# DeltaNet query norms through VectorE block transposes, stacked meta values, and one meta product per attention head

## The chip, the cores and the metric

The kernel runs on one core of one Trainium2 chip. The metric is the device time of one launch in microseconds (us). The engines are named as the profile names them: PE (TensorE matmuls), PEld (its weight loads), DVE (VectorE), ACT (ScalarE), POOL (GpSimd) and SP (SyncE, which issues DMAs here).

## The reference, cut to what matters

One layer of a hybrid decoder: RMS norm, one combined input projection (2048 channels, 512 tokens and 16 meta tokens ahead of them), three token mixers on disjoint heads, a gate on each head, one output projection, a residual and a last norm. The change touches two of the mixers.

```python
q_dn = l2_normalize(to_heads(cq, DN_HEADS)) * DN_DK ** -0.5      # t * rsqrt(sum(t*t) + EPS)
k_dn = l2_normalize(to_heads(ck, DN_HEADS))
o_dn = gated_delta_rule_chunked(q_dn, k_dn, v_dn, log_a, beta)   # solves (I + A) per chunk
o_dn = gated_head_norm(o_dn, dz, dn_norm_w)                      # o * rsqrt(mean(o*o) + EPS) * w * silu(z)
...
logits = einsum('bhqd,bhkd->bhqk', q_i, k) + c_i[..., :, None] - c[:, :, None, :]
mask = (key_pos <= q_pos) & (key_pos >= PAD)                     # the 16 meta tokens are keys too
o_fox = einsum('bhqk,bhkd->bhqd', softmax(where(mask, logits, NEG)), v)
```

DeltaNet has 6 heads of 128 channels, the forgetting attention 5 heads of 128. A query's square sum over its 128 channels is needed per head and token: 6 x 512 numbers.

## The kernel before, in words

The input projection is one long stream of PE matmuls. Float32 weights arrive by DMA as `raw` tiles (128x1024), ACT rounds them to a high part (`whi`, the cast at L167), DVE subtracts to get the low part (`wlo`, the split at L168), and each 128x128 piece is multiplied three times (xh by whi, xl by whi, xh by wlo; L235). A block is one such tile against 512 token columns (24 matmuls) or against 528 in two halves (48). There are 131 such casts and splits. PE can't begin a block's `wlo` products before its split is done.

DeltaNet works in two groups g = 0 and 1 of H = 3 heads. For each group the program has `dn_keys` (L655-713), `dn_inverse` (L716 on), `dn_values` (L811), `dn_queries` and `dn_mix` (L835 on). Queries lie as `qT`, channels in the partitions, so the square sum of a query crosses partitions. Before, each of the four 128-token blocks transposed its three heads' queries on PE (`pq`, L878) and ACT squared the result with an accumulated sum (L881); then an Ln and an Exp gave the reciprocal (L935, L936). `dn_inverse` inverts 51 matrices of 32x32 by a chain of 60 small DVE steps (L737 a product, L741 an addition, in place in `ab`), writes the result out and reads it back in another layout by DMAs that ACT issues (L744, L745 to the scratch `sc`; L748, L750 back as `iv` and `xm`), transposes 32x32 blocks on DVE (L755), and goes on with small PE products (`pm` L761, `pl`, `pn`). `conv_silu` makes keys, values and queries: `pb` from PSUM (L356), a four-tap convolution on DVE (L600, L602), then `silu`: a clamp on POOL (L367), three ACT steps (L368 to L370) and a DVE product (L371). A gate head goes from PSUM through L385 and the same `silu`.

A forgetting-attention head adds the meta tokens' share to its output `pfo` last. Probabilities of the meta keys lie as `ptm` (ACT copies L1271), the values as `vm` inside the tile `fm` in a high and a low part, side by side (L1176, L1177), and two 128x512 matmuls add them (L1279).

The order on each engine is made when the program is built, by a list scheduler that runs over a modelled timeline. Casts and splits have high priority. Some pieces are pinned: `behind(mm, n)` puts a PE product behind the n-th next product of the stream, and a `waits` list puts DVE's transposes of the inverse (L755) behind a given split. Every engine then runs its list in order, so whatever stands behind a waiting instruction waits too.

Of the kernel before, what the change touches and what calls it, by code (L numbers as in the profile page):

```python
# [8 lines left out]
F32 = mybir.dt.float32  # L9
# [5 lines left out]
ALU = mybir.AluOpType  # L15
# [68 lines left out]
def tile_hybrid_trunk(ctx, tc, xT, x_first, w_first, xtok, mtok, w_gate, w_in, w_out, w_dn, consts, lmask, fin_w, out, dbg=None):  # L84
# [16 lines left out]
    def t15(name, shape=(P, H, P), dt=F32):  # L101
        return wk.tile(list(shape), dt, tag="t15", bufs=6, name=name)
# [532 lines left out]
    def dn_keys(g):  # L635
# [19 lines left out]
        G.memset(kdm, 0.0)  # L655
        anm = wk.tile([NM, H, NM], F32, tag="anm", bufs=1, name=f"anm{g}")
        atm = wk.tile([NM, H, NM], F32, tag="atm", bufs=1, name=f"atm{g}")
        cols = wk.tile([P, 4, 5, H], F32, tag="cols", name=f"cols{g}")
        nb2, br, nbg, tmp = (cols[:, i] for i in range(4))
        gcl = lambda b, j: gcol[:NM if b == 4 else P, b, 6 + H * g + j : 6 + H * g + j + 1]  # L660
        G.memset(sk, 1.0)
        for b in (4, 0, 1, 2, 3):
# [35 lines left out]
        for b in (4, 0, 1, 2, 3):  # L698
# [10 lines left out]
            for j in range(H):  # L709
                dst = an[:, b * H + j, :] if b < 4 else anm[:, j, :]  # L710
                V.scalar_tensor_tensor(out=dst, in0=pg[:r, j * r : (j + 1) * r], scalar=nb2[:r, b, j : j + 1],
                                       in1=e2[:r, j, :r], op0=ALU.mult, op1=ALU.mult)
        st.update(kT=kT, kd=kd, at=at, an=an, kdm=kdm, anm=anm, br=br, nbg=nbg)
        return st

    def dn_inverse(g, st):  # L716
# [93 lines left out]

    def dn_values(g, st):  # L811
        vp = six.tile([P, NN, P], F32, tag="six", name=f"vp{g}")
        vpm = t15(f"vpm{g}", (P, P))
        G.memset(vpm, 0.0)
        br = st["br"]
        for j in range(H):
            h = H * g + j
            v = row(f"v{h}")[:, :T]
            conv_silu(("dv", h), 12 + h, v)
            pv = psm.tile([P, 512], F32, tag="m", name=f"pv{h}")  # L820
            for b in range(NB):
                PE.transpose(pv[:, b * P : (b + 1) * P], v[:, bsl(b)], ident)
            for b in range(NB):
                V.tensor_scalar_mul(vp[:, b * H + j, :], pv[:, b * P : (b + 1) * P], br[:, b, j : j + 1])
            pv2 = psm.tile([P, 512], F32, tag="m", name=f"pvm{h}")
            PE.transpose(pv2[:NM, :P], v[:, 0:NM], ident)
            V.tensor_scalar_mul(vpm[32 * j : 32 * j + NM], pv2[:NM, :P], br[:NM, 4, j : j + 1])
        st.update(vp=vp, vpm=vpm)

    def dn_queries(g, st):  # L830
# [5 lines left out]
    def dn_mix(g, st):  # L836
# [14 lines left out]
        f_ = wk.tile([P, 2, NB, H], F32, tag="ff", name=f"ff{g}")  # L851
        egs, egls, ons = {}, {}, {}

        def gated(b):
            pt = psm.tile([P, 512], F32, tag="m", name=f"pt{g}{b}")
            for j in range(H):
                PE.transpose(pt[:, j * P : (j + 1) * P], ons[b][:, j, :], ident)
            for j in range(H):
                o = zs["dz", H * g + j][:, b * P : (b + 1) * P]
                V.scalar_tensor_tensor(out=o, in0=pt[:, j * P : (j + 1) * P], scalar=dnws[:, 0:1], in1=o,  # L860
                                       op0=ALU.mult, op1=ALU.mult)
# [9 lines left out]
        def scores(b):  # L871
            ts = bsl(b)
            p1 = psm.tile([P, 512], F32, tag="m", name=f"pa{g}{b}")
            p2 = psm.tile([P, 512], F32, tag="m", name=f"pq{g}{b}")
            for j in range(H):
                PE.matmul(p1[:, j * P : (j + 1) * P], kT[:, j, ts], qT[:, j, ts], start=True, stop=True)
            for j in range(H):
                PE.transpose(p2[:, j * P : (j + 1) * P], qT[:, j, ts], ident)  # L878
            for j in range(H):
                sq = wk.tile([P, P], BF16, tag="sq", name=f"sqq{g}{b}{j}")  # L880
                A.activation(sq, p2[:, j * P : (j + 1) * P], AF.Square, accum_out=sq_[:, b, j : j + 1])  # L881
            atb = at[:, b * H : b * H + H, :]
            V.tensor_tensor(out=atb, in0=p1[:, : H * P].rearrange("p (h d) -> p h d", h=H), in1=atb, op=ALU.mult)
            eg = t15(f"eg{g}{b}")
            nc.sync.dma_start(out=eg, in_=gd[6 + H * g : 6 + H * g + H, ts].partition_broadcast(P))
            A.activation(eg, eg, AF.Exp)
            egl = wk.tile([P, H], F32, tag="egl", name=f"egl{g}{b}")
            V.tensor_copy(egl, eg[:, :, P - 1])
            G.tensor_tensor(out=eg, in0=eg, in1=qT[:, :, ts], op=ALU.mult)
            egs[b], egls[b] = eg, egl  # L890

        scores(0)
        for b in range(NB):
            ts, eg, egl = bsl(b), egs[b], egls[b]
            pk = psm.tile([P, 512], F32, tag="m", name=f"pks{g}{b}")
            for j in range(H):
                mm = PE.matmul(pk[:, j * P : (j + 1) * P], kT[:, j, ts], sst[:, j, :], start=True, stop=True)
            soon(mm, b, 0)
            z = t15(f"zz{g}{b}")
            for j in range(H):  # L900
                V.scalar_tensor_tensor(out=z[:, j, :], in0=pk[:, j * P : (j + 1) * P], scalar=nbg[:, b, j : j + 1],
                                       in1=vp[:, b * H + j, :], op0=ALU.mult, op1=ALU.add)
            py = psm.tile([P, 512], F32, tag="m", name=f"py{g}{b}")
            for j in range(H):
                mm = PE.matmul(py[:, j * P : (j + 1) * P], uf[:, b * H + j, :], z[:, j, :], start=True, stop=True)
                if j == 0:
                    late(mm, b, 1)
            soon(mm, b, 1)
            y = t15(f"y{g}{b}")
            A.copy(y, py[:, : H * P].rearrange("p (h d) -> p h d", h=H))  # L910
            if b < NB - 1:
                pn = psm.tile([P, 512], F32, tag="m", name=f"psn{g}{b}")
                for j in range(H):
                    mm = PE.matmul(pn[:, j * P : (j + 1) * P], kd[:, b * H + j, :], y[:, j, :], start=True, stop=True)
                    if j == 0:
                        late(mm, b, 2)
                soon(mm, b, 2)
                sn = t15(f"sn{g}{b}")
                for j in range(H):
                    V.scalar_tensor_tensor(out=sn[:, j, :], in0=sst[:, j, :], scalar=egl[:, j : j + 1],  # L920
                                           in1=pn[:, j * P : (j + 1) * P], op0=ALU.mult, op1=ALU.add)
                scores(b + 1)
            if b:
                gated(b - 1)
            po = psm.tile([P, 512], F32, tag="m", name=f"po{g}{b}")
            for j in range(H):
                pj = po[:, j * P : (j + 1) * P]
                PE.matmul(pj, at[:, b * H + j, :], y[:, j, :], start=True, stop=False)
                PE.matmul(pj, eg[:, j, :], sst[:, j, :], start=False, stop=True)
            for j in range(H):  # L930
                sq = wk.tile([P, P], BF16, tag="sq", name=f"sqo{g}{b}{j}")
                A.activation(sq, po[:, j * P : (j + 1) * P], AF.Square, accum_out=so_[:, b, j : j + 1])

            f1, f2 = f_[:, 0, b, :], f_[:, 1, b, :]
            A.activation(f1, sq_[:, b, :], AF.Ln, bias=eps_c)  # L935
            A.activation(f2, f1, AF.Exp, scale=-1.0)  # L936
            V.tensor_tensor(out=f2, in0=f2, in1=so_[:, b, :], op=ALU.mult)
            A.activation(f2, f2, AF.Ln, scale=1.0 / (P * P), bias=eps_c)
# [220 lines left out]
    def fox_head(h):  # L1159
# [5 lines left out]
        def values(v):  # L1165
# [7 lines left out]
            A.copy(v3, pv[:, 3 * P :])  # L1173
            pw = psm.tile([P, 512], F32, tag="m", name=f"pwf{h}")
            PE.transpose(pw[:, :P], v4, ident)
            A.copy(vm[:, 0], pw[:, :P])  # L1176
            V.tensor_tensor(out=vm[:, 1], in0=pw[:, :P], in1=vm[:, 0].bitcast(F32), op=ALU.subtract)  # L1177
            return vhi, vlo

        if h < H1:  # L1180
# [35 lines left out]
            G.affine_select(out=o, in_=i, pattern=[[0, o.shape[1]], [-1, P]], base=0, channel_multiplier=1,  # L1216
                            compare_op=ALU.is_ge, fill=BIG)
        fm = t15(f"fm{h}", dt=F32R)
        vm, mt = fm[:, 0:2], fm[:, 2].rearrange("p (b i t) -> p b i t", b=NB, i=2)
        hi, lo = (six.tile([P, 3, T], F32R, tag="six", name=f"fp{n}{h}") for n in ("hi", "lo"))  # L1220
        for t in (hi, lo):
            V.memset(t[:, 0, 0:1].bitcast(F32), 0.0)
# [45 lines left out]
        PE.transpose(pw[:, :P], fm[:, 2].bitcast(F32), ident)  # L1268
        for b in range(NB):
            r, bs = slice(32 * b, 32 * b + 32), slice(b * P, (b + 1) * P)  # L1270
            A.copy(pm[r, bs], pw[r, :P])  # L1271
        po = psm.tile([P, 512], F32, tag="m", name=f"pfo{h}")
        for jb in range(3):
            js, qs = slice(jb * P, (jb + 1) * P), slice(jb * P, S)
            for i, (v_, p_) in enumerate(((vhi, hi), (vhi, lo), (vlo, hi))):
                PE.matmul(po[:, qs], v_[:, js], p_[:, jb, qs], start=(jb + i == 0), stop=False)  # L1276
        PE.matmul(po[:, 3 * P :], v3, p3, start=False, stop=False)
        for i in range(2):
            PE.matmul(po, vm[:, i], pm, start=False, stop=i == 1)  # L1279
        V.tensor_tensor(out=z, in0=po[:, :512], in1=z, op=ALU.mult)  # L1280
        if h < FOX_HEADS - 1:
            nc.sync.dma_start(out=zd[DN_HEADS + GLA_HEADS + h], in_=z)
# [397 lines left out]
```

## Time and profile before

| | |
|---|---|
| runs | 974.40, 972.32, 972.87 us (median 972.87) |
| profiled execution | 972.28 us, span 970.6 us |
| PE busy | 960.8 us (99% of the span) |
| DVE busy | 673.0 us (69%) |
| ACT busy | 476.4 us (49%) |
| POOL busy | 221.2 us (23%) |
| `pq` transposes, L878 | 24 matmuls, 239.4 to 458.2 us |
| meta products of attention, L1279 | 10 matmuls, 674.6 to 835.3 us |

A matmul's duration in a row includes its passage through the pipeline; two neighbours overlap. What a matmul costs PE is therefore read from the start of one to the start of the next.

### The profile page before, as it was taken

What the parts mean: (1) busy time and instruction counts of PE and PEld (TensorE: products, weight loads), DVE (VectorE), ACT (ScalarE), POOL (GpSimd) and SP (SyncE); (2) the same over time, 40 slices, a digit from 0 to 9 for tenths busy, and PEclk for the clock granted to TensorE, in tenths of its full rate; (3) what the DMA queues carried; (4) which work ended last, traced back from release to release, by engine and by line L of the source; (5) the groups of instructions that cost most, each with busy time, mean ns of one, the idle gap of its engine ahead of it and who ended that gap; (6) DMA issues with size and microseconds to landing.
All of it is one profiled execution on the core that took longest, in us unless ns stands there. A gap on an engine that the chain in (4) does not pass through costs nothing.

```text
span 970.6 us, 18917 instructions
## 1 busy us (share of the span) xinstructions
PE 960.8 (99%) x7301; PEld 885.2 (91%) x7301; DVE 673.0 (69%) x1463; ACT 476.4 (49%) x1046; POOL 221.2 (23%) x243
## 2 busy tenths in 40 slices
PE   9999999999999999999999999999999999999996
PEld 7899999899999878899999989899999998888885
DVE  6467767877658886434685957867867768977664
ACT  7754433345356233334545545555555545644345
POOL 0032322232123225111213223223332120000033
PEclk9999999999999999999999999999999999999998
DMA  9736677988558687734647575688775587366535
GB/s 353 297 135 208 195 195 213 283 230 224 176 151 232 208 237 196 192 106 104 166 129 189 147 195 172 182 227 210 205 207 163 177 288 273 131 209 222 182 126 174
DMA packets 70336, 191.87 MB, mean 198 GB/s; under 512 B 14078, under 2 KB 17326, under 8 KB 69477
## 3 DMA queue, kind: packets, MB, share of 16 engines
q1 hardware_dynamic: 46048, 152.64, 45.4%
q0 software_dynamic: 15104, 31.66, 18.2%
q10 hardware_dynamic: 9092, 6.36, 2.4%
q8 instruction: 57, 0.93, 0.4%
q14 instruction: 35, 0.28, 0.1%
HBM read 179.94 MB, written 60.88 MB: 248 GB/s over the span
## 4 chain that ended last, share of the span: by engine, by line
PE 98%; DVE 1%; issue 0%; DMA 0%; ACT 0%; SPq 0%; DVEq 0%
PE pp L235 49%; PE pp_a L560 8%; PE pq L1401 6%; PE pp L314 5%; PE pa L1401 3%; PE pt L1401 3%; PE ps L1401 3%; PE pp_c L560 2%; PE pp_d L560 2%; PE pp_b L560 2%; PE pr L1401 1%; PE pss L1046 1%; PE pfo L1276 1%; PE pgate L408 1%; PE pfa L1228 1%; PE pg L704 1%
## 5 line engine op out<-in xcount | busy, mean ns | idle before, releaser
L235 PE MATMUL pp<-xh,wlo 128*128 128x264 f32 (+2 forms) x1120 | 270.0, 305 | 0.0
L235 PE MATMUL pp<-xl,whi 128*128 128x264 f32 (+2 forms) x1120 | 269.6, 305 | 0.0
L235 PE MATMUL pp<-xh,whi 128*128 128x264 f32 (+2 forms) x1120 | 269.5, 305 | 0.0
L167 ACT CAST whi<-raw 128x1024 fp32r<-128x1024 f32 x131 | 137.2, 1047 | 179.5 <-PE pp L235 110.1
L168 DVE TENSOR_TENSOR wlo<-raw,whi 128x1024 fp32r<-128x1024 f32 x131 | 160.6, 1226 | 59.5 <-ACT whi L167 50.1
L235 PEld LDWEIGHTS pp<-xh,wlo 128*128 128x128 f32 x1120 | 181.5, 189 | 9.2 <-DVE wlo L168 0.7
L235 PEld LDWEIGHTS pp<-xh,whi 128*128 128x128 f32 x1120 | 181.3, 188 | 8.7 <-issue 0.2
L235 PEld LDWEIGHTS pp<-xl,whi 128*128 128x128 f32 x1120 | 181.6, 189 | 8.2
L367 POOL TENSOR_SCALAR stc<-cv 128x528 f32<-128x528 f32 (+1 forms) x18 | 27.2, 1513 | 132.0 <-DVE cv L602 120.9
L602 DVE SCALAR_TENSOR_TENSOR cv<-pb,cpk,cv 128x528 f32<-128x528 f32 (+1 forms) x54 | 40.9, 757 | 0.8
L1430 POOL TENSOR_TENSOR acc<-acc,fw 128x512 f32<-128x512 f32 x4 | 6.1, 1544 | 138.4 <-DVE wll L168 138.4
L168 DVE TENSOR_TENSOR wlos<-raws,whis 128x1024 fp32r<-128x1024 f32 x20 | 24.3, 1223 | 15.0 <-ACT whis L167 15.0
L167 ACT CAST whis<-raws 128x1024 fp32r<-128x1024 f32 x20 | 20.7, 1050 | 28.2 <-PE ps L1401 9.2
L314 PE MATMUL pp<-xh,wf 128*128 128x512 f32 x128 | 33.1, 398 | 0.3 <-ACT wf L291 0.3
L314 PEld LDWEIGHTS pp<-xh,wf 128*128 128x128 f32 x128 | 24.2, 190 | 6.1 <-ACT wf L291 0.6
L560 PE MATMUL pp_a<-t,whi 128*128 128x264 f32 (+1 forms) x224 | 29.4, 282 | 0.0
L356 DVE TENSOR_TENSOR pb<-pp,rstd 128x264 f32<-128x264 f32 (+1 forms) x36 | 13.8, 425 | 22.1 <-PE pp L235 22.0
L560 PE MATMUL pp_a<-xl,whi 128*128 128x264 f32 x112 | 28.4, 288 | 0.0
L560 PE MATMUL pp_a<-xh,whi 128*128 128x264 f32 x112 | 28.1, 285 | 0.0
L560 PEld LDWEIGHTS pp_a<-t,whi 128*128 128x128 f32 x224 | 27.6, 188 | 0.0
L474 POOL DMA_DIRECT2D tw<-tw x16 | 13.4, 837 | 60.9 <-DVE wlo L168 29.5
L1401 PE MATMUL pq<-whia,a 128*128 128x512 f32 x80 | 25.5, 394 | 0.0
(487 smaller groups left out, 2058.2 us busy)
## 6 DMA issues: line engine op xcount, KB each, us to landing
raw<-in_w_in SPq DMA_DIRECT2D x103, 512.0 KB, 3.9
ti<-in_w_in SPq DMA_DIRECT2D x28, 512.0 KB, 5.4
raw<-ti SPq DMA_DIRECT2D x28, 512.0 KB, 3.4
tw<-in_w_dn SPq DMA_DIRECT2D x20, 512.0 KB, 5.3
raws<-tw SPq DMA_DIRECT2D x15, 512.0 KB, 3.7
ti<-in_w_in POOLq DMA_DIRECT2D x14, 512.0 KB, 7.0
ti<-ti POOLq DMA_DIRECT2D x14, 512.0 KB, 6.7
tw<-in_w_dn POOLq DMA_DIRECT2D x10, 512.0 KB, 6.7
```

Source lines behind the costliest of these rows:

```text
L167: pace[0] = A.copy(hi, raw).ins
L168: pace[1] = V.tensor_tensor(out=lo, in0=raw, in1=hi.bitcast(F32), op=ALU.subtract).ins
L235: mm = PE.matmul(p_[:, :nt], wt[:, j * m : (j + 1) * m], xx[k][:, t0 : t0 + nt], start=(k == 0 and wt is hi and xx is xh), stop=(k == KT - ...
L314: PE.matmul(begun[i][0][0][:, :S], wt[:, i * P : (i + 1) * P], xx[k][:, NM:T], start=k + n == 0, stop=k == KT - 1 and n == 2)
L356: V.tensor_tensor(out=o, in0=p_[rows], in1=rstd[rows, t0 : t0 + n], op=ALU.mult)
L367: maxes.append(G.tensor_scalar_max(t, src, LOW).ins)
L408: PE.matmul(pgate[a][:, :HT], wg[k // 8][:, k % 8, :], xx[k][:, a * HT : (a + 1) * HT], start=(k == 0 and xx is xh), stop=(k == KT - 1 and ...
L474: x = G.dma_start(out=out_[s], in_=in_[s], accum_op=ALU.add, max_dma_last_dim=2048)
L560: m = PE.matmul(p_[:, cols], wt[:, j * P : (j + 1) * P], xx[j][part_][:, cols], start=first and i == 0, stop=i == len(todo) - 1, skip_grou ...
L602: V.scalar_tensor_tensor(out=c, in0=pb[:, t0 + w : w + T], scalar=cwc[:, blk, w : w + 1], in1=c, op0=ALU.mult, op1=ALU.add)
L704: PE.matmul(pg[:r, j * r : (j + 1) * r], kT[:, j, ts], kT[:, j, ts], start=True, stop=True)
L1401: mm = PE.matmul(p_, o_[:, s], w_, start=(first and n == 0), stop=(last and n == 2), skip_group_check=True)
```

## The change: what it does

Three things, in the diff below.

1. `query_sums`, once per group, takes the place of the four `pq` parts. For each head DVE transposes the 32x32 blocks of `qT` (128x512) into a `row` tile `qs`, POOL squares it in place, DVE sums 32 neighbours (128x512 to 128x16) into `qsum`. One PE product with a fold matrix adds what lies in the four groups of 32 partitions (`pq`, 128x48), ACT copies it into place in four pieces, and one Ln and one Exp serve all four blocks.
2. The values' meta tokens are copied by POOL side by side into one tile (`vms`), and one 128x128 PE transpose and one DVE product replace three of each. The fold matrix is made here, from the identity, in a third of the same tile, which now lives until `pq`.
3. The attention heads stack the high and the low part of the meta values in partitions 0 to 31 and 32 to 63. POOL copies the probabilities to the partitions 32 to 63 (L1294 of the changed kernel) and one matmul replaces two.

```diff
         def query_sums():
+            sums = wk.tile([P, H, 16], F32, tag="qsum", bufs=1, name=f"qsum{g}")
+            for j in range(H):
+                t = row(f"qs{H * g + j}")[:, :S]
+                V.transpose(t, qT[:, j, NM:])
+                G.tensor_tensor(out=t, in0=t, in1=t, op=ALU.mult)
+                V.reduce_sum(sums[:, j], t.rearrange("p (m b) -> p m b", b=32), axis=mybir.AxisListType.X)
+            pq = psm.tile([P, 512], F32, tag="m", name=f"pq{g}")
+            PE.matmul(pq[:, : 16 * H], st["fold"], sums.rearrange("p h m -> p (h m)"),
+                      start=True, stop=True)
+            for i in range(4):
+                r = slice(32 * i, 32 * i + 32)
+                A.copy(sq_[r], pq[r, : 16 * H].rearrange("p (h b i) -> p b h i", h=H, i=4)[:, :, :, i])
+            A.activation(f_[:, 0], sq_, AF.Ln, bias=eps_c)
+            A.activation(f_[:, 1], f_[:, 0], AF.Exp, scale=-1.0)
...
             for j in range(H):
                 PE.matmul(p1[:, j * P : (j + 1) * P], kT[:, j, ts], qT[:, j, ts], start=True, stop=True)
-            for j in range(H):
-                PE.transpose(p2[:, j * P : (j + 1) * P], qT[:, j, ts], ident)
-            for j in range(H):
-                sq = wk.tile([P, P], BF16, tag="sq", name=f"sqq{g}{b}{j}")
-                A.activation(sq, p2[:, j * P : (j + 1) * P], AF.Square, accum_out=sq_[:, b, j : j + 1])
...
             A.copy(y, py[:, : H * P].rearrange("p (h d) -> p h d", h=H))
+            if b == 0:
+                query_sums()
...
-            A.activation(f1, sq_[:, b, :], AF.Ln, bias=eps_c)
-            A.activation(f2, f1, AF.Exp, scale=-1.0)
...
+        vpm3 = t15(f"vpm{g}")
+        vpm = vpm3[:, 0]
+        vms = vpm3[:, 1]
+        G.memset(vms, 0.0)
+        fold = vpm3[:, 2].rearrange("p (i a) -> p i a", i=4)
+        V.reduce_sum(fold[:, 0], ident.rearrange("p (i a) -> p a i", a=32), axis=mybir.AxisListType.X)
+        V.tensor_copy(fold[:, 1:], fold[:, 0].unsqueeze(1).to_broadcast([P, 3, 32]))
...
-            PE.transpose(pv2[:NM, :P], v[:, 0:NM], ident)
-            V.tensor_scalar_mul(vpm[32 * j : 32 * j + NM], pv2[:NM, :P], br[:NM, 4, j : j + 1])
+            G.tensor_copy(vms[:, 32 * j : 32 * j + NM], v[:, 0:NM])
+        pv2 = psm.tile([P, 512], F32, tag="m", name=f"pvm{g}")
+        PE.transpose(pv2[:, :P], vms, ident)
+        V.tensor_scalar_mul(vpm, pv2[:, :P], brm)
...
-            A.copy(vm[:, 0], pw[:, :P])
-            V.tensor_tensor(out=vm[:, 1], in0=pw[:, :P], in1=vm[:, 0].bitcast(F32), op=ALU.subtract)
+            A.copy(vm, pw[:, :P])
+            V.tensor_tensor(out=vm[32:64], in0=pw[32:64, :P], in1=vm[32:64].bitcast(F32), op=ALU.subtract)
...
-            A.copy(pm[r, bs], pw[r, :P])
+            A.copy(pm[0:32, bs], pw[r, :P])
+        G.tensor_copy(pm[32:64], pm[0:32].bitcast(F32))
...
-        for i in range(2):
-            PE.matmul(po, vm[:, i], pm, start=False, stop=i == 1)
+        PE.matmul(po, vm, pm, start=False, stop=True)
```

The new DVE and POOL steps have no wait on the mixing block that their code stands in, only on the queries, and the scheduler places them much earlier. Three places show it. Rows are those of the built programs, in the order in which an engine runs them; rows of the changed kernel carry its own line numbers (L870 the block transpose, L871 the square, L872 the sum, L874 the fold product).

First, DVE at the end of the inverse of g = 0. `ab` is the inverse's tile, `pb` and `cv` are the convolution of a key head of the next group, `pp` the projection's PSUM. Before:

```order
L741 TENSOR_TENSOR ab_2040<-ab_2040 51x3x28
L737 TENSOR_TENSOR ab_2040<-ab_2040 51x58
L741 TENSOR_TENSOR ab_2040<-ab_2040 51x2x29
L737 TENSOR_TENSOR ab_2040<-ab_2040 51x30
L741 TENSOR_TENSOR ab_2040<-ab_2040 51x30
L356 TENSOR_TENSOR pb_2673<-pp_0_2675,rstd 128x264
L356 TENSOR_TENSOR pb_2673<-pp_1_2676,rstd 128x264
L600 TENSOR_SCALAR cv_2790<-pb_2673,cpk 128x528
L168 TENSOR_TENSOR wlo_1_2864<-raw_1_2860,whi_1_2863 128x1024
```

The same place in the changed kernel:

```order
L741 TENSOR_TENSOR ab_2043<-ab_2043 51x3x28
L356 TENSOR_TENSOR pb_2649<-pp_0_2651,rstd 128x264
L737 TENSOR_TENSOR ab_2043<-ab_2043 51x58
L356 TENSOR_TENSOR pb_2649<-pp_1_2652,rstd 128x264
L741 TENSOR_TENSOR ab_2043<-ab_2043 51x2x29
L600 TENSOR_SCALAR cv_2766<-pb_2649,cpk 128x528
L168 TENSOR_TENSOR wlo_1_2840<-raw_1_2836,whi_1_2839 128x1024
L737 TENSOR_TENSOR ab_2043<-ab_2043 51x30
L602 SCALAR_TENSOR_TENSOR cv_2766<-pb_2649,cpk,cv_2766 128x528
L741 TENSOR_TENSOR ab_2043<-ab_2043 51x30
```

The last four steps of the inverse now stand behind `pb`, which waits for the projection, and the last two behind a split as well.

Second, DVE and POOL at the start of the inverse of g = 1. `zgz` is a gate head on its way from PSUM, `qT` the last query head, `stc` and `stgz` the clamped copies inside `silu`, `ti` a weight prefetch. DVE before:

```order
L741 TENSOR_TENSOR ab_4048<-ab_4048 51x28x3
L737 TENSOR_TENSOR ab_4048<-ab_4048 51x108
L741 TENSOR_TENSOR ab_4048<-ab_4048 51x27x4
L737 TENSOR_TENSOR ab_4048<-ab_4048 51x130
L371 TENSOR_TENSOR qT_3665<-cv_4037,stc_4042 128x512
L741 TENSOR_TENSOR ab_4048<-ab_4048 51x26x5
L385 TENSOR_TENSOR zgz_4599<-pp_0_4535,rstd 128x512
L737 TENSOR_TENSOR ab_4048<-ab_4048 51x150
L168 TENSOR_TENSOR wlo_1_4644<-raw_1_4640,whi_1_4643 128x1024
```

DVE of the changed kernel, from the inverse's second step to the same split:

```order
L741 TENSOR_TENSOR ab_4027<-ab_4027 51x30
L872 TENSOR_REDUCE qsum_4252<-qs_4253 128x16
L737 TENSOR_TENSOR ab_4027<-ab_4027 51x58
L371 TENSOR_TENSOR qT_3644<-cv_4016,stc_4021 128x512
L741 TENSOR_TENSOR ab_4027<-ab_4027 51x29x2
L872 TENSOR_REDUCE qsum_4252<-qs_4257 128x16
L870 STREAM_TRANSPOSE qs_4261<-qT_3644 128x512
L737 TENSOR_TENSOR ab_4027<-ab_4027 51x84
L385 TENSOR_TENSOR zgz_4551<-pp_0_4487,rstd 128x512
L168 TENSOR_TENSOR wlo_1_4596<-raw_1_4592,whi_1_4595 128x1024
```

POOL of the changed kernel at that place (before, the three rows of L871 were not there):

```order
L732 MEMSET ab_4027 51x32
L367 TENSOR_SCALAR stc_4021<-cv_4016 128x512
L871 TENSOR_TENSOR qs_4253<-qs_4253 128x512
L871 TENSOR_TENSOR qs_4257<-qs_4257 128x512
L479 DMA ti<-ti 256x512
L871 TENSOR_TENSOR qs_4261<-qs_4261 128x512
L367 TENSOR_SCALAR stgz_4553<-zgz_4551 128x512
```

Two sums that wait for POOL's squares, one block transpose, the gate head and fewer steps of the inverse now stand between the inverse's start and that split; the gate head's clamp stands behind the third square.

Third, PE in the first mixing block of g = 0. Before, the three transposes stood behind the scores `pa`; now the one fold product stands later, behind `py`:

```order
L846 MATMUL ps_2231<-ym_2229,kdm_1058 128x128 x3
L876 MATMUL pa_2240<-qT_1658,kT_670 128x128 x3
L878 MATMUL pq_2241<-ident,qT_1658 128x128 x3
L235 MATMUL pp_0_3245<-xh_312,wlo_1_3306 128x264
```

```order
L927 MATMUL py_2262<-zz_2258,uf_2183 128x128 x3
L874 MATMUL pq_2281<-qsum_2268,vpm_1235 128x48
L235 MATMUL pp_0_3366<-xh_150,wlo_0_3372 128x264
L235 MATMUL pp_1_3367<-xh_150,wlo_0_3372 128x264
```

The places of `pm`, `pl` and `pn` in the stream, counted in products of the stream, are the same in both.

More of the change, by code (lines that the diff above doesn't have):

```diff
@@ L657, in dn_keys @@
         atm = wk.tile([NM, H, NM], F32, tag="atm", bufs=1, name=f"atm{g}")
-        cols = wk.tile([P, 4, 5, H], F32, tag="cols", name=f"cols{g}")
-        nb2, br, nbg, tmp = (cols[:, i] for i in range(4))
+        cols = wk.tile([P, 4 * 5 * H + 1], F32, tag="cols", name=f"cols{g}")
+        nb2, br, nbg, tmp = (cols[:, 5 * H * i : 5 * H * i + 5 * H].rearrange("p (b h) -> p b h", h=H) for i in range(4))
         gcl = lambda b, j: gcol[:NM if b == 4 else P, b, 6 + H * g + j : 6 + H * g + j + 1]
@@ L712, in dn_keys @@
                                        in1=e2[:r, j, :r], op0=ALU.mult, op1=ALU.mult)
-        st.update(kT=kT, kd=kd, at=at, an=an, kdm=kdm, anm=anm, br=br, nbg=nbg)
+        st.update(kT=kT, kd=kd, at=at, an=an, kdm=kdm, anm=anm, br=br, nbg=nbg, brm=cols[:, 20 * H :])
         return st
@@ L812, in dn_values @@
         vp = six.tile([P, NN, P], F32, tag="six", name=f"vp{g}")
-        vpm = t15(f"vpm{g}", (P, P))
-        G.memset(vpm, 0.0)
+        vpm3 = t15(f"vpm{g}")
[5 more added lines that the diff above has]
+        V.tensor_copy(fold[:, 1:], fold[:, 0].unsqueeze(1).to_broadcast([P, 3, 32]))
+        st["fold"] = vpm3[:, 2]
         br = st["br"]
+        brm = st["brm"]
+        G.memset(brm, 0.0)
+        for j in range(H):
+            V.tensor_copy(brm[32 * j : 32 * j + NM], br[:NM, 4, j : j + 1])
         for j in range(H):
@@ L824, in dn_values @@
                 V.tensor_scalar_mul(vp[:, b * H + j, :], pv[:, b * P : (b + 1) * P], br[:, b, j : j + 1])
-            pv2 = psm.tile([P, 512], F32, tag="m", name=f"pvm{h}")
-            PE.transpose(pv2[:NM, :P], v[:, 0:NM], ident)
-            V.tensor_scalar_mul(vpm[32 * j : 32 * j + NM], pv2[:NM, :P], br[:NM, 4, j : j + 1])
+            G.tensor_copy(vms[:, 32 * j : 32 * j + NM], v[:, 0:NM])
+        pv2 = psm.tile([P, 512], F32, tag="m", name=f"pvm{g}")
+        PE.transpose(pv2[:, :P], vms, ident)
+        V.tensor_scalar_mul(vpm, pv2[:, :P], brm)
         st.update(vp=vp, vpm=vpm)
@@ L852, in dn_mix, with query_sums @@
         egs, egls, ons = {}, {}, {}
+        def query_sums():
+            sums = wk.tile([P, H, 16], F32, tag="qsum", bufs=1, name=f"qsum{g}")
+            for j in range(H):
+                t = row(f"qs{H * g + j}")[:, :S]
[10 more added lines that the diff above has]
+            A.activation(f_[:, 1], f_[:, 0], AF.Exp, scale=-1.0)
         def gated(b):
@@ L873, in scores @@
             p1 = psm.tile([P, 512], F32, tag="m", name=f"pa{g}{b}")
-            p2 = psm.tile([P, 512], F32, tag="m", name=f"pq{g}{b}")
             for j in range(H):
                 PE.matmul(p1[:, j * P : (j + 1) * P], kT[:, j, ts], qT[:, j, ts], start=True, stop=True)
-            for j in range(H):
-                PE.transpose(p2[:, j * P : (j + 1) * P], qT[:, j, ts], ident)
-            for j in range(H):
-                sq = wk.tile([P, P], BF16, tag="sq", name=f"sqq{g}{b}{j}")
-                A.activation(sq, p2[:, j * P : (j + 1) * P], AF.Square, accum_out=sq_[:, b, j : j + 1])
             atb = at[:, b * H : b * H + H, :]
@@ L1218, in fox_head @@
         fm = t15(f"fm{h}", dt=F32R)
-        vm, mt = fm[:, 0:2], fm[:, 2].rearrange("p (b i t) -> p b i t", b=NB, i=2)
+        vm, mt = fm[:, 0], fm[:, 2].rearrange("p (b i t) -> p b i t", b=NB, i=2)
         hi, lo = (six.tile([P, 3, T], F32R, tag="six", name=f"fp{n}{h}") for n in ("hi", "lo"))
```

## The prediction

> **What bounds the kernel now.** I read the page's busy shares and its chain first, then PE's waits.
>
> ```profile
> PE 960.8 (99%) x7301; PEld 885.2 (91%) x7301; DVE 673.0 (69%) x1463; ACT 476.4 (49%) x1046; POOL 221.2 (23%) x243
> PEclk9999999999999999999999999999999999999998
> PE 98%; DVE 1%; issue 0%; DMA 0%; ACT 0%; SPq 0%; DVEq 0%
> PE warm L303 <- POOL ones L115: 1.2, 1, 1.2
> PE pp L314 <- ACT wf L291: 0.3, 1, 0.3
> PE pfx L1246 <- DVE fm L1241: 0.2, 1, 0.2
> ```
>
> PE is busy from end to end at full clock, and its waits add up to 1.7 us. So two questions decide: how many PE steps go, and whether any step PE needs comes later than PE does. Everything taken from ACT is worth nothing by itself.
>
> **What PE loses.** The query transposes and the meta products:
>
> ```profile
> 239.39 0.49 PE L878 MATMUL pq<-ident,qT 128*128 128x128 f32 x3
> 239.64 0.49 PE L235 MATMUL pp<-xh,wlo 128*128 128x264 f32 x2
> L878 PE MATMUL pq<-ident,qT x24: 272/273/273, 239.4 to 458.2; 128*128 128x128 f32 x24
> 674.60 0.72 PE L1279 MATMUL pfo<-ptm,fm 128*128 128x512 f32 x2
> 675.16 0.28 PE L560 MATMUL pp_b<-xl,whi 128*128 128x264 f32 x1
> ```
>
> Three transposes take 0.25 us from start to start (not the 0.273 us of each, most of which is pipeline), so 24 take 8 x 0.25 = 2.0 us here and up to 2.6 where the last of three is followed by a fresh group (0.33 per three); I take 2.4. Two meta products take 0.56 us, one in a running stream 0.23 (343.42 to 343.65, below): 5 x 0.23 to 0.28, taken as 1.2. Added are two fold products, 128x48 in float32; the nearest row is the transpose at 0.08 each, the upper bound one 128x512 product at 0.28, so 0.2 to 0.5, taken as 0.3. The stacked meta values replace six narrow transposes by two full ones: at 0.08 each that is between -0.3 and +0.2, taken as 0. Sum: -2.4 - 1.2 + 0.3 = **-3.3 us** (-2.7 to -3.7).
>
> **What ACT loses and gains.** The squares (L881, 24 pairs) and per-block Ln and Exp go, four copies and one Ln and Exp per group come. PE waits for ACT once, at L291, so this is worth 0; it hides behind PE and would cost nothing with that cover gone, being a removal. In attention, the POOL copy to partitions 32 to 63 comes behind ACT's four copies:
>
> ```profile
> 668.71 1.05 ACT L1271 CAST ptm<-pfw 32x128 fp32r<-32x128 f32 x4
> ```
>
> They end at 669.76, the product that needs them starts at 674.60: 4.8 us for a copy of 32x512. POOL's dearest 128x512 step below takes 3.35, so 0; without the cover 0.6 to 3.4 us for each of five heads.
>
> **What DVE and POOL gain, and what stands behind it.** Per group three block transposes, three sums on DVE, three squares on POOL. A transpose of 128x384 took 0.58 (row at 214.19 below), so 128x512 is some 0.77. A sum isn't in the trace; it reads 512 columns as L600 does (0.49), the three-operand L371 takes 0.68: I take 0.6. That is 3 x 1.37 = 4.1 us of DVE per group, in the inverse's chain. A POOL square is bounded by these:
>
> ```profile
> L1430 POOL TENSOR_TENSOR accs<-accs,fw 128x512 f32<-128x512 f32 x8 | 10.1, 1294 | 0.0
> L1070 POOL TENSOR_TENSOR gt<-gt,gqk 128x512 f32<-128x512 f32 x2 | 6.7, 3353 | 20.2 <-ACT gt L1069 20.2
> 182.28 2.70 POOL L367 TENSOR_SCALAR stdz<-zdz 128x512 f32<-128x512 f32 x1 [4.11 <-DVE zdz L385]
> 183.55 0.81 DVE L741 TENSOR_TENSOR ab<-ab 51x240 f32<-51x240 f32 x1
> 184.40 0.40 DVE L737 TENSOR_TENSOR ab<-ab 51x240 f32<-51x240 f32 x1
> ```
>
> 1.3 alone, 3.35 at worst. Beside the inverse's steps a POOL clamp takes 2.70 where the same takes 1.49 alone (336.86 below), and one step of the chain 0.81 where its twin takes 0.40. So: 1.3 for a square while DVE waits for it, some 1.8 beside DVE, and about 0.4 back to DVE for each.
>
> *End of the inverse, g = 0.*
>
> ```profile
> 202.24 0.18 DVE L741 TENSOR_TENSOR ab<-ab 51x30 f32<-51x30 f32 x1
> 204.10 0.77 DVE L356 TENSOR_TENSOR pb<-pp,rstd 128x264 f32<-128x264 f32 x2 [1.68 <-PE pp L235]
> 205.39 1.22 DVE L168 TENSOR_TENSOR wlo<-raw,whi 128x1024 fp32r<-128x1024 f32 x1
> 202.45 0.32 ACTq L744 DMA_DIRECT2D sc<-ab  x1
> 207.82 0.39 ACTq L748 DMA_DIRECT2D iv<-sc  x1
> 213.53 0.63 DVE L755 STREAM_TRANSPOSE um<-xm 32x32 f32<-32x32 f32 x3 [0.69 <-DMA xm<-sc]
> 214.19 0.58 DVE L755 STREAM_TRANSPOSE iv<-iv 128x384 f32<-128x384 f32 x1
> DMA to landing us min/median/max: 5.4/5.6/5.8
> 218.29 0.95 PE L761 MATMUL pm<-iv,an 32*32 32x32 f32 x48
> 373.40 0.32 ACTq L744 DMA_DIRECT2D sc<-ab  x1
> 376.30 0.39 ACTq L748 DMA_DIRECT2D iv<-sc  x1
> ```
>
> Before, the chain ends at 202.42, goes out and back in two hops (5.4 us to 207.82, then 5.4 to 5.8, the landing row of L748) and is transposed by 214.77: 3.5 us ahead of `pm`. Now its last steps stand behind `pb`, which PE releases at 204.10 at the earliest, and behind a split. From there: 0.77 for `pb`, two steps 0.4, L600 0.49, the split 1.22, a step 0.2, L602 0.75, the last 0.2: 208.1; with 4.1 us of new DVE work less the 1.7 us that DVE idled there, up to 209.5. Then 5.4 + 5.4 + 0.6 gives `iv` at 219.5 to 220.9, PE waits 1.2 to 2.6. The first hop is the unknown: for g = 1 it took 2.9 (373.40 to 376.30), which would make the wait 0; and with 5.8 for the second, 3.0 us. I take **+1.5**, nearest the g = 0 rows. Late next are ACT's copies of `iv` and the cast queued behind them; the split after it comes equally late, so it adds no wait of its own. For g = 1 the two rows are far apart:
>
> ```profile
> 385.22 0.58 DVE L755 STREAM_TRANSPOSE iv<-iv 128x384 f32<-128x384 f32 x1
> L761 PE MATMUL pm<-iv,an x96: 191/191/212, 218.3 to 396.0; 32*32 32x32 f32 x96
> ```
>
> The second use of `pm` runs to 396.0, some 10 us behind the transpose, which covers 5 of slip: 0.
>
> *Start of the inverse, g = 1.*
>
> ```profile
> 336.76 0.20 DVE L737 TENSOR_TENSOR ab<-ab 51x30 f32<-51x30 f32 x1 [1.70 <-DMA ab<-scr]
> 336.86 1.49 POOL L367 TENSOR_SCALAR stc<-cv 128x512 f32<-128x512 f32 x1
> 342.00 1.21 DVE L168 TENSOR_TENSOR wlo<-raw,whi 128x1024 fp32r<-128x1024 f32 x1
> 343.42 0.39 PE L235 MATMUL pp<-xl,whi 128*128 128x512 f32 x1
> 343.65 0.40 PE L235 MATMUL pp<-xh,wlo 128*128 128x512 f32 x1
> 342.02 2.54 POOL L367 TENSOR_SCALAR stgz<-zgz 128x512 f32<-128x512 f32 x1 [2.77 <-DVE zgz L385]
> 347.95 1.21 DVE L168 TENSOR_TENSOR wlo<-raw,whi 128x1024 fp32r<-128x1024 f32 x1
> 349.22 0.50 PE L235 MATMUL pp<-xh,wlo 128*128 128x512 f32 x1
> ```
>
> The first two block transposes stand where DVE waited 1.7 us for `ab`, at no cost. The split of 342.00 ends at 343.21 and its first product starts at 343.65; the next ends at 349.16 for 349.22, 24 products of 0.232 later. There is 0.4 and 0.06 us of room, the tightest place I found. Now the first sum waits for the first square, which stands behind the clamp that ends at 338.35: 339.65. Then sum 0.6, step 0.2, L371 0.6, step 0.2 (341.3), the second sum (its square is done by about 341.4) 0.6, transpose 0.77, step 0.25, gate head 0.6, split 1.2: 344.9. PE waits 1.25. The third square runs to about 344.9, the gate's clamp to 347.2, two ACT steps and the cast (1.3 + 1.05) to 349.6, the split to 350.8, against 344.9 + 5.57 = 350.5: 0.3 more. I take **+1.5**; 0.5 if sum and transpose are half my figures, 4.3 with squares of 2.5 us (second sum at 343.4, split to 346.8, next split to 353.5).
>
> Elsewhere the new steps have room. In the middle of the inverse of g = 0:
>
> ```profile
> 182.42 1.21 DVE L168 TENSOR_TENSOR wlo<-raw,whi 128x1024 fp32r<-128x1024 f32 x1
> 186.61 0.39 PE L235 MATMUL pp<-xh,wlo 128*128 128x512 f32 x1
> ```
>
> The split ends 3.0 us ahead of its first product and, by the same steps as above, comes some 2 later; with squares of 3.35 us it would be short by 1. In the mixing blocks products come 0.25 us sooner, which I count as covered.
>
> Sum: 972.28 - 3.3 + 1.5 + 1.5 = 972.0, rounded up for what I didn't find: **972.1**. The profiled execution lies 0.6 below the median of the runs, so against the median the saving is 0.1%. About 0.2% (1.9 us) is what a measurement here tells from no change.
>
> **Rivals.**
> 1. *The waits are small.* The first hop takes 2.9 and the sums are quick: 972.28 - 3.3 + 0 + 0.5 = 969.5. For it: the g = 1 hop, and that both waits rest on durations estimated here. Against: POOL's queue in front of the first square is in the order, whatever the sum costs.
> 2. *POOL's squares and DVE hold each other up (slower).* Place: the second and third square at 339.7 us, and all three of g = 0. Price: squares of 2.5 us, 4.3 at the start of g = 1 and 2.6 at the end of g = 0: 972.28 - 3.3 + 6.9 = 975.9. It decides from squares of 1.9 us up. For it: the 2.70 and 2.54 clamps beside the chain, L1070's 3.35. Against: in 2.70 us of clamp DVE lost only one 0.4. The Trainium skill (SBUF - State Buffer, section on the two separate sides) calls the port pair shared by VectorE and GpSimd an exclusive lock: a two-input VectorE step or a GpSimd step holds it for a whole instruction, and the other blocks fully. By that rule each square would cost the chain its own 1.3 us in place of 0.4, some 2.7 us more per group and an estimate of 974.7 to 977 us; the 0.81 row agrees with blocking but not with a whole instruction lost.
> 3. *The meta products don't come free.* If POOL's copy waited behind its clamps in all five heads, 0.6 us each would eat the 1.2 saved and 1.8 more: 973.8. Against it the 4.8 us of room; it is also where the change would not do what it says.
>
> **How the numbers follow.** The forecast (saving given back by two waits) has 0.47, of which 0.06 falls below -0.2% and 0.03 above +0.2%; rival 1 has 0.27, all faster; rival 2 0.21, of which 0.04 within 0.2%; rival 3 0.05, within 0.2% but for 0.01. That makes faster 0.06 + 0.27, same 0.38 + 0.04 + 0.04, slower 0.03 + 0.17 + 0.01. The forecast's own range is 970.3 to 973.8. Leaving a tenth out at each end takes in most of both rivals: 968.9 to 975.4.
>
> **What would show it.** Right: `pq` on PE twice, 0.1 to 0.25 us; L1279's successor five times; PE waits at `pm` near 218 us and at `wlo` near 343 us, 1 to 2 us each, in PE's list of waits; iv's DMA issued after 213. Squares (L871) of 1.3 to 2.1 us. Wrong: no wait at either place (rival 1), squares above 2.5 and steps of the inverse doubled (rival 2), a PE wait ahead of the last `pfo` product (rival 3), or a new wait in a mixing block, for which I have given no price.

## The result, and the profile after

The changed kernel took 975.81 us (median of 15 runs, 973.08 to 979.56) against 972.35 for the kernel before (15 runs, 971.05 to 974.40): ratio 1.0041, 95% interval 1.0029 to 1.0054. It is slower by 0.4%. The forecast was 972.1, its range ended at 975.4, and "slower" had 0.21. One run of experiment 3 (1437.89 us) and one of experiment 4 (1040.28 us) lie far outside their fellows and are left out of the ratios below.

The profiled execution is one of the longer ones, 978.29 us (span 976.6), 6.0 above the profiled execution of before. Its page, in the parts that answer to those shown of before (busy time, granted clock in 40 slices, the chain that ended last):

```profile
PE 960.0 (98%) x7272; PEld 884.4 (91%) x7272; DVE 679.5 (70%) x1481; ACT 469.5 (48%) x994; POOL 235.7 (24%) x262
...
PEclk9999999998999999999999999999999999999999
...
PE 82%; DVE 7%; DMA 5%; issue 3%; ACT 1%; POOL 1%; ACTq 0%; POOLq 0%; DVEq 0%
```

PE was alone on the chain before (98%). Now the tenth slice has a lower clock, and DVE, DMA and issue stand on the chain with 15% together. PE's waits (total, times, longest) name the places:

```profile
PE pm L761 <- DVE iv L755: 4.7, 1, 4.7
PE pp L235 <- DVE wlo L168: 1.2, 1, 1.2
PE warm L303 <- POOL ones L115: 1.2, 1, 1.2
PE pfx L1268 <- DVE fm L1263: 1.1, 1, 1.1
```

The first two are the two places of the forecast. The second is 1.4 us when read from the start of one product to the start of the next; ahead of it a sum on DVE waits for POOL's square, as forecast (timelines of DVE and PE):

```profile
345.42 0.69 DVE L872 TENSOR_REDUCE qsum<-qs 128x16 f32<-128x512 f32 x1 [1.87 <-POOL qs L871]
...
350.75 0.51 PE L235 MATMUL pp<-xh,wlo 128*128 128x512 f32 x1 [1.24 <-DVE wlo L168]
```

The first is three times as long as forecast. The timeline of DVE, ACT, POOL and PE there (start, duration, engine, line):

```profile
204.80 0.42 DVE L356 TENSOR_TENSOR pb<-pp,rstd 128x264 f32<-128x264 f32 x1
...
206.20 1.22 DVE L168 TENSOR_TENSOR wlo<-raw,whi 128x1024 fp32r<-128x1024 f32 x1
...
208.12 0.17 DVE L741 TENSOR_TENSOR ab<-ab 51x30 f32<-51x30 f32 x1
208.32 0.32 ACTq L744 DMA_DIRECT2D sc<-ab  x1
...
213.30 0.95 POOL L479 DMA_DIRECT2D ti<-in_w_in  x1
213.98 0.39 ACTq L748 DMA_DIRECT2D iv<-sc  x1
...
217.82 0.28 PE L235 MATMUL pp<-xl,whi 128*128 128x264 f32 x1
222.16 0.58 DVE L755 STREAM_TRANSPOSE iv<-iv 128x384 f32<-128x384 f32 x1 [10.26 <-DMA iv<-sc]
222.79 1.49 PE L761 MATMUL pm<-iv,an 32*32 32x32 f32 x48 [4.69 <-DVE iv L755]
...
225.03 0.64 PE L235 MATMUL pp<-xh,whi 128*128 128x264 f32 x2
225.47 0.64 PE L235 MATMUL pp<-xl,whi 128*128 128x264 f32 x2
```

The chain of the inverse ends at 208.29, behind `pb` and a split. The way out takes 5.7 us (208.32 to 213.98), the way back 8.2 (213.98 to 222.16); before it took 5.4. POOL's weight prefetch `ti` was issued 0.7 us ahead of it; before, POOL issued it 2.8 us behind. When PE goes on, two products of 128x264 take 0.44 us from start to start in place of 0.24. By the microsecond (window, its length, PE busy, granted clock, DMA share, GB/s):

```profile
220.00:221.00 1.00, 0.00 (x0) 1.00 1.12 359
221.00:222.00 1.00, 0.00 (x0) 0.76 0.85 325
222.00:223.00 1.00, 0.21 (x8) 0.50 0.28 114
...
227.00:228.00 1.00, 1.00 (x6) 0.50 0.00 0
228.00:229.00 1.00, 1.00 (x9) 0.83 0.00 0
```

The 0.76 and the 0.83 are windows that lie partly at 1.00 and partly at 0.50, so the clock is at half from about 221.5 to 228.3. That costs `pm` 0.54 us (1.42 from its start to the next product, 0.88 before) and the products behind it some 1.85: 2.4 together.

The sum of the two profiled executions then closes. Removed products, from start to start over all their rows, took 5.39 us (`pq` 2.46, `pvm` 0.16, meta products 2.77); those in their place take 1.84 (0.29, 0.06, 1.50): 3.55 saved. Against it stand 4.7 at `pm`, 2.4 for the clock, 1.4 at the split near 349 us and 0.8 more than before at `pfx`: +5.75, measured +6.0.

### The profile page after: what moved, and what is told of

Read it like the earlier page. It is cut to its first block, busy times and chain, and to the rows that moved or that the text cites. A ratio compares the mean times of both kernels' runs of the same rounds, so it can differ in the third digit from the quotient of the medians.

```text
span 976.6 us, 18856 instructions
## 1 busy us (share of the span) xinstructions
PE 960.0 (98%) x7272; PEld 884.4 (91%) x7272; DVE 679.5 (70%) x1481; ACT 469.5 (48%) x994; POOL 235.7 (24%) x262
## 4 chain that ended last, share of the span: by engine, by line
PE 82%; DVE 7%; DMA 5%; issue 3%; ACT 1%; POOL 1%; ACTq 0%; POOLq 0%; DVEq 0%
PE pp L235 39%; PE pp_a L560 7%; PE pp L314 5%; PE pq L1423 4%; PE pt L1423 3%; PE pa L1423 3%; PE ps L1423 3%; PE pp_c L560 2%; PE pp_d L560 2%; DVE wlo L168 2%; PE pp_b L560 2%; PE pr L1423 1%; PE pss L1068 1%; DMA iv<-sc 1%; PE pgate L408 1%
## 5 line engine op out<-in xcount | busy, mean ns | idle before, releaser
L167 ACT CAST whi<-raw 128x1024 fp32r<-128x1024 f32 x131 | 137.2, 1047 | 162.0 <-PE pp L235 94.3
L167 ACT CAST whis<-raws 128x1024 fp32r<-128x1024 f32 x20 | 20.8, 1050 | 27.9 <-PE pq L1423 9.1
L911 POOL TENSOR_TENSOR eg<-eg,qT 128x384 f32<-128x384 f32 x8 | 8.1, 1012 | 76.4 <-DVE egl L910 38.6
```

What stands on the lines that cost most here:

```text
L167: pace[0] = A.copy(hi, raw).ins
```

## The experiments

Each is compared with the kernel before, run beside it. Intervals are 95%.

**1. Without the query sums.** The query transposes and the squares on ACT are put back, the other two parts stay.

```diff
-            if b == 0:
-                query_sums()
+            for j in range(H):
+                PE.transpose(p2[:, j * P : (j + 1) * P], qT[:, j, ts], ident)
+            for j in range(H):
+                A.activation(sq, p2[:, j * P : (j + 1) * P], AF.Square, accum_out=sq_[:, b, j : j + 1])
...
+            A.activation(f1, sq_[:, b, :], AF.Ln, bias=eps_c)
+            A.activation(f2, f1, AF.Exp, scale=-1.0)
```

> Edit: the query transposes and squares of the kernel before are put back; the stacked meta values and the single meta product per attention head stay. Theory L (the loss comes from the new DVE and POOL steps making the inverse late: in the profile after, PE waits 4.7 us for iv at pm, runs some 2.5 us worth of products slowly behind that wait, waits 1.3 us for a split near 349 us and 0.8 us more than before at pfx, against 3.5 us of PE work saved): the waits at pm and at the split are gone, PE saves 1.4 us (meta products and narrow transposes), time 970.5 to 971.5, ratio 0.998 to 0.999. Rival O (the other parts or the changed order at large cost the time): slower than before, 974 or more.

971.47 us, ratio 0.9992 (0.9983 to 1.0001): between the expected gain and no difference. PE doesn't wait at `pm`. `pfx` waits 1.0 us here too, so that wait isn't the sums' doing. The loss lies in the query sums or in the order that they brought.

**2. The product pinned later.** `PM, SP = (308, 340)` becomes `(356, 340)`: `pm` and what follows it stand 48 stream products later.

> Edit: the changed kernel with the inverse's first PE product of group 0 (and what follows it) pinned 48 stream products (5.9 us) later; all else the same. Theory L: iv is there when PE comes, no wait at pm, the granted clock stays at 1.00 there; the waits at the split near 349 us (1.3) and pfx (about 1) stay: 972.3 - 3.5 + 1.3 + 0.8 = 970.9, range 970 to 972, some 5 us under the changed kernel. Rival D (the lateness is only handed on to pl, uf and the first mixing block, which stand at the same distance): new waits there, 974 or more.

980.06 us, ratio 1.0080 (1.0066 to 1.0093): slower than the changed kernel. The lateness was handed on, though not to the consumer that I had named. The timeline of ACT and PE there:

```profile
222.24 2.07 ACT L780 COPY uf<-iv 32x384 f32<-32x384 f32 x4 [2.96 <-DMA gb<-gd]
224.33 1.99 ACT L167 CAST whi<-raw 128x1024 fp32r<-128x1024 f32 x2
225.43 0.51 PE L235 MATMUL pp<-xh,whi 128*128 128x264 f32 x2 [4.46 <-ACT whi L167]
```

ACT's copies of `iv` (L780) stand ahead of a weight cast (L167) in ACT's order. They wait for `iv` (the row names another DMA, but the transpose of `iv` ends at 222.15, just ahead of them), and the stream's next block waits for the cast. Where `pm` stands makes no difference to that; only an earlier `iv` helps.

**3. The old order at one place.** The changed kernel, with `pb` of the next key head pinned behind the last step of the inverse of g = 0.

```diff
-        evac(inproj(key, first=0 if meta else NM - 4), pb, off=3)
+        pins = evac(inproj(key, first=0 if meta else NM - 4), pb, off=3)
+        for x in pins if key == ("dk", 3) else ():
+            tc.add_manual_dep(x, ended[0].name, mybir.DependencyInfo(
+                mybir.DependencyClass.NoSync, mybir.DependencyReason.DATA), reason="behind")
```

> Edit: the changed kernel, but the key head's convolution input (pb of the first key head of group 1) may not run ahead of the last step of group 0's inverse, as in the kernel before; block transposes, squares and sums stay where they are. Theory L with the order as the cause: the chain ends near 205.7 us in place of 208.3, PE waits 0 to 2 us at pm and the clock holds: 970.5 to 972.5. Rival S (the 4 us of new DVE work and the squares' blocking by themselves make the chain late): the chain ends at 207.5 or later, the wait at pm stays above 3 us, 974.5 to 977.

970.17 us, ratio 0.9979 (0.9970 to 0.9988): 5.6 us under the changed kernel's median, and faster than before. The timeline of DVE, ACT and POOL from the end of the chain on (its lines are 8 to 9 further down):

```profile
205.60 0.18 DVE L749 TENSOR_TENSOR ab<-ab 51x30 f32<-51x30 f32 x1
205.71 1.23 DVE L168 TENSOR_TENSOR wlo<-raw,whi 128x1024 fp32r<-128x1024 f32 x1
205.81 0.32 ACTq L753 DMA_DIRECT2D sc<-ab  x1
...
209.40 0.39 ACTq L757 DMA_DIRECT2D iv<-sc  x1
...
212.32 0.94 POOL L482 DMA_DIRECT2D ti<-in_w_in  x1
214.02 0.58 DVE L764 STREAM_TRANSPOSE iv<-iv 128x384 f32<-128x384 f32 x1
```

The chain ends at 205.78, as expected, with all the new DVE and POOL steps still in it. The way back leaves at 209.40, ahead of the prefetch, and takes 4.6 us. PE waits nowhere near 218 us.

So `iv` is there 8.1 us earlier than in the changed kernel: 2.5 us come from the chain's end, 2.1 from a shorter way out (3.6 us against 5.7, for which no run isolates a reason) and 3.5 from a shorter way back. The chain still ends 3.4 us later than before. That is what the new steps cost it by themselves, and it makes PE wait for nothing here. The other 2.5 us are the order: in the changed kernel's profile DVE came to `pb` at 204.80 without waiting, and the steps put ahead of the chain's last four took that time.

**4. The squares on ACT.** `G.tensor_tensor(out=t, in0=t, in1=t, op=ALU.mult)` becomes `A.activation(t, t, AF.Square)`.

> Edit: the three squares per group run on ACT in place of POOL, so POOL no longer holds DVE up beside them; DVE's transposes and sums stay. Rival S (POOL's squares, 1.7 to 2.8 us each beside DVE, and the DVE steps stretched to 1.2 us beside them, are the cause): the chain of group 0 ends 2 us or more earlier, no wait above 1 us at pm, 971 or less. Theory L with the order as the cause: the last steps of the chain still stand behind pb and a split, the chain ends at 207 or later, the wait at pm stays 3 us or more in most runs: 973.5 to 976; the wait at the split near 349 us shrinks below 0.5.

975.94 us, ratio 1.0041 (1.0027 to 1.0055), the changed kernel's own time. The chain ends at 207.64 (DVE's timeline), its last steps behind `pb` and a split as in the changed kernel:

```profile
207.46 0.18 DVE L741 TENSOR_TENSOR ab<-ab 51x30 f32<-51x30 f32 x1
```

And PE waits at `pm` (list of its waits):

```profile
PE pm L761 <- DVE iv L755: 3.7, 1, 3.7
```

The wait at the split near 349 us is gone. The stretch from the first step of that inverse to the end of that split took 6.45 us before, 7.95 in the changed kernel and 6.95 here, so POOL's squares made some 1.0 of the added 1.5 us. Whether PE then waits depends on when the inverse starts, too: in experiments 6 and 7 the stretch is 7.96 us, with POOL's squares, and PE doesn't wait there. The rival that POOL's squares decide the whole falls.

**5. The new order alone.** The kernel before, without any of the change, but the last two pairs of the inverse's steps stand behind `pb` and the first convolution step. PE's and SP's orders are those of before.

```diff
+        for a, b in ((steps[0, 29], pins[0]), (steps[0, 30], x)) if key == ("dk", 3) else ():
+            tc.add_manual_dep(a, b.name, mybir.DependencyInfo(
+                mybir.DependencyClass.NoSync, mybir.DependencyReason.DATA), reason="behind")
```

> Edit: the kernel before with nothing of the change but its order at one place: the last two pairs of steps of group 0's inverse stand behind pb and the first convolution step of the next key head, as in the changed kernel; no block transposes, no squares, no sums, PE's order is unchanged. Theory L (this order is what costs): the chain ends at 206.8 to 208.2 us in place of 202.4, iv's second hop is issued after 212 and takes 5.5 to 8.5, PE waits 1 to 5 us at pm and, where that is above some 3.5, loses 2.5 more to the clock: 974 to 979, slower than before. Rival S (the 4 us of new DVE steps are needed for the loss): within 1 us of before.

978.20 us, ratio 1.0046 (1.0030 to 1.0063). Three of twelve runs lie at 971.2 to 973.7, nine at 977.4 to 978.9. The profiled one is among the nine; its timeline of DVE, POOL, ACT and PE:

```profile
203.91 0.43 DVE L357 TENSOR_TENSOR pb<-pp,rstd 128x264 f32<-128x264 f32 x1 [2.61 <-PE pp L235]
...
207.24 0.18 DVE L750 TENSOR_TENSOR ab<-ab 51x30 f32<-51x30 f32 x1
...
212.43 0.95 POOL L482 DMA_DIRECT2D ti<-in_w_in  x1
213.02 0.39 ACTq L757 DMA_DIRECT2D iv<-sc  x1
...
221.56 0.58 DVE L764 STREAM_TRANSPOSE iv<-iv 128x384 f32<-128x384 f32 x1 [9.60 <-DMA iv<-sc]
222.19 1.44 PE L770 MATMUL pm<-iv,an 32*32 32x32 f32 x46 [4.03 <-DVE iv L764]
```

DVE waits 2.6 us for PE at `pb` while four short steps of the chain stand behind it. In nine of the twelve runs this order is enough by itself for the whole loss; none of the new arithmetic is needed. Why three runs escape it was not profiled.

**6. The wait filled.** The changed kernel, with products whose result nobody reads in front of `pm`.

```diff
+        if g == 0:
+            pf = psm.tile([P, 512], F32, tag="m", name="fill")
+            for i in range(36):
+                behind(PE.matmul(pf[:, :P], ident, ident, start=True, stop=True), PM[g])
```

> Edit: the changed kernel with 36 float32 products of 128x128 into a PSUM tile that nobody reads (some 4 us of PE work) placed in front of pm of group 0, where PE waits in most runs. If the slow products behind the wait come from PE standing still for more than some 3.5 us, the clock stays at 1.00 there and the 2.5 us come back where the wait was 4.7: about 973 to 974.5, the wait at pm 0 to 1.5 us. If the slow products have another cause, the time is the changed kernel's or worse (976 to 980).

981.67 us, ratio 1.0099 (1.0086 to 1.0112). I had mis-sized the filling: in the trace the 36 products are 72 matmuls, and they took 8.1 us, not 4. PE's timeline:

```profile
217.72 8.20 PE L760 MATMUL fill<-ident 128*128 128x128 f32 x72
...
233.41 0.24 PE L774 MATMUL pl<-iv 32*32 32x32 f32 x2 [3.23 <-ACT iv L769]
```

So the time says nothing about the clock; the windows do (columns as above):

```profile
220.00:225.00 5.00, 5.00 (x48) 1.00 0.49 171
225.00:230.00 5.00, 5.00 (x83) 1.00 0.24 81
...
231.00:232.00 1.00, 0.00 (x0) 1.00 0.01 0
...
235.00:236.00 1.00, 1.00 (x5) 0.50 0.90 162
...
237.00:238.00 1.00, 1.00 (x6) 0.50 0.38 82
```

With PE kept busy, the clock stayed at 1.00 where the changed kernel had 0.50. A wait of 3.2 us then arose at `pl`, behind ACT, and behind that wait the clock fell to 0.50 again.

**7. The prefetch held back.** The changed kernel, but POOL's prefetch that stood just ahead of the way back waits until `iv` is transposed.

```diff
+    tc.add_manual_dep(pool_dmas[9], turned[0].name, mybir.DependencyInfo(
+        mybir.DependencyClass.Sync, mybir.DependencyReason.DATA), reason="held")
```

> Edit: the changed kernel, but the one weight prefetch that POOL issues just ahead of iv's read (at 213.30 us in the profile after) waits until iv is transposed. If it is this prefetch that makes iv's hop 8 us in place of 5.5, the hop takes 5 to 6.5 us, PE waits 1.5 to 3 us at pm and the clock holds: 971 to 973.5. If the hop is slow for another reason (SP's two prefetches, the small packets themselves), it stays at 7.5 to 8.5 and the time at 975 to 978.

972.97 us, ratio 1.0005 (0.9995 to 1.0014): 2.8 us under the changed kernel. The profiled execution is the longest of the twelve, 975.19 us. Its timeline of ACT, DVE and PE:

```profile
213.95 0.39 ACTq L752 DMA_DIRECT2D iv<-sc  x1
...
219.64 0.58 DVE L759 STREAM_TRANSPOSE iv<-iv 128x384 f32<-128x384 f32 x1 [7.81 <-DMA iv<-sc]
220.27 0.95 PE L766 MATMUL pm<-iv,an 32*32 32x32 f32 x48 [2.23 <-DVE iv L759]
```

And by the microsecond (columns as above):

```profile
222.00:223.00 1.00, 1.00 (x7) 0.50 0.73 102
...
225.00:226.00 1.00, 1.00 (x9) 0.99 0.15 25
```

The way back was issued at the same time as in the changed kernel and took 5.7 us in place of 8.2. So this one prefetch, 512 KB, makes the difference. The other profiled executions agree: where the prefetch was issued 0.15 to 0.7 us ahead of the way back (the changed kernel, experiments 2, 4, 5 and 6), the way back took 8.0 to 8.6 us; where it came 1.8 us or more behind (the kernel before, experiments 1, 3 and 8), 2.9 to 5.6. Not expected: the clock fell to half here too, after a wait of 2.2 us and the 0.9 us of small products of `pm` behind it. That cost some 1.5 us.

**8. Experiments 3 and 4 together.**

> Edit: both of the earlier edits at once: pb of the next key head behind the inverse's last step, and the squares on ACT. PE keeps the saving of 3.5 us, nothing waits at pm, the split near 342 us comes in time, and pfx is what it is: 968.5 to 970, ratio 0.996 to 0.998. If ACT's new work or DVE's sums make another split late, no better than the first of the two edits (970.2).

970.85 us, ratio 0.9987 (0.9978 to 0.9996). Its waits at the split and at `pfx` are gone, and another of 0.9 us stands near 625 us (PE `pp_a` for ACT's `vf`). It is no better than experiment 3, and the two intervals overlap.

## Why the prediction was wrong, point by point

- **PE's saving: right.** 3.3 forecast, 3.55 measured. The 5 meta products fell by 1.27 (forecast 1.2), the fold products cost 0.29 (0.3).
- **DVE's and POOL's new steps: right for DVE, too small for POOL.** A block transpose took 0.69 (0.77 forecast), a sum 0.67 (0.6). POOL's squares took 2.2, 1.2 and 2.8 in group 0 and 1.0 each in group 1. Beside those of group 0 three steps of the inverse took 1.1 to 1.2 in place of 0.4, so a square cost the chain some 0.8 and not the 0.4 that I took. (The clamp of 1.49 that I called alone ran beside steps of the inverse, too.) Two squares exceed the 1.9 from which rival 2 was to decide; experiment 4 shows that it doesn't.
- **The chain's end, g = 0: right.** 208.1 to 209.5 forecast from the order and the rows, 208.29 measured. The lower figure let PE's release of `pb` decide; in the profile DVE's chain was already 3.4 us later than before when it reached `pb`, by the new work, and `pb` didn't wait for PE.
- **The wait at `pm`: the term that failed, +1.5 forecast, 7.1 in the profiled execution (4.7 of waiting and 2.4 of slow products).** Two things were missing. First, I carried over the way back at 5.4 to 5.8 us. The chain's slip moved that DMA from ahead of POOL's prefetch to right behind it, and it took 8.2; experiment 7 shows that this prefetch is the reason. The prediction had read the duration, not what else is issued at the new time. Second, the term had no price for the clock. The prediction took a wait to cost its own length; 2.4 us more followed. The Trainium skill (TensorE: Matmul & The Clock Gate, Part 1) says that PE's clock is halved after about 3.4 us of idle; the trace agrees in the changed kernel, where it fell some 3.4 us into the wait of 4.7. Other runs differ: in experiment 5 it fell some 2.5 us into the wait, and in experiment 7 it fell after a wait of 2.2 us.
- **"The split after it comes equally late": right, and stronger than I used it.** Experiment 2 shows that ACT's copies and the cast behind them set the same lateness, wherever `pm` stands.
- **The start of the inverse, g = 1: right in place and size.** 1.5 forecast, 1.4 measured, though everything there ran 6 us later than I drew it. The first sum waits for POOL's square and PE for the split, as forecast. Experiment 4 gives back 1.0 of the 1.5 us. That PE waited for nearly all of it is in part luck: in experiments 6 and 7 it waited for none. I had split the 1.5 into 1.25 at this split and 0.3 at the next, where PE didn't wait. (My steps up to the split add up to 344.8, not 344.9.)
- **The cause named in rival 2 (POOL's squares): wrong.** The side was right and the mechanism wasn't: the order at one place costs the time without any square (experiment 5).
- **Attention: rival 3 fell.** POOL's copy takes 0.6 us and no product waits for it. (Its sum was wrong, too: with the 1.2 saved given back and 1.8 more lost, 972.0 becomes 975.0, not 973.8.) The 0.8 us at `pfx` had no price in the prediction. It arises with and without the sums (experiment 1) and is missing in experiments 4, 5, 6 and 8; in the trace a DVE step (L1262) of 0.23 takes 1.32 beside a POOL product, at the same place where another DVE step was stretched before. What set the timing was not tried.
- **Chances.** The cases were made by mechanisms that each ended at their rows' own bounds. The pieces that add up on one path (late chain, slower hop, clock) were never added: 208.3 + 5.7 + 8.2 + 0.6 = 222.8, 4.7 behind PE, and 2.4 on top.

What stays open: how often the way back is slow, what shortened the way out in experiment 3, and how long a wait has to be for the clock to fall. The changed kernel's runs spread over 6.5 us where those of before spread over 3.4, and those of experiment 5 fall into two groups; that this is the hop's length and the clock's step is likely from the profiled executions, but only they show the hop.

## What to carry to other kernels

A list scheduler answers a small change with a new order, and one short chain that slips behind longer or waiting instructions can cost more than the change saves: look first at which dependent chains gained a long or a waiting neighbour, and for each slipped DMA at what is issued around its new time. Repairing that one place (experiment 3) turned 0.4% slower into 0.2% faster. Where one engine is busy all the time, a wait of some microseconds (2.2 us and more here) costs its length and can bring a stretch of half clock with it.

## What the runs showed of the hardware that was not expected

- The half clock lasted 3.4 us after waits of 2.2 us (221.6 to 225.0, experiment 7) and 3.2 us (experiment 6), each followed by 48 small products, and 6.8 us with the wait of 4.7; the wait of 1.2 us at the split near 349 us left it at 1.00 in the windows around. The bounds are estimates from the windows' mean clocks.
- The clock's fall came at no fixed distance from PE's stop: some 2.5 us after PE stopped in experiment 5 (granted clock 0.81 from 220 to 221 us, PE idle since 218.2), 3.4 in the changed kernel, and 5.2 in experiment 2 (0.58 from 226 to 227, PE idle from 221.0 to 225.4).
- A read of 192 KB in small pieces took 5.7 or 8.2 us, depending on one 512 KB prefetch from POOL's queue issued 0.7 us ahead of it (experiment 7 against the changed kernel).
